# Loading the second tile of an early output projection ahead of the values, and pacing the first tile closer, in a hybrid attention layer

## The chip, the cores and the metric

The kernel runs on one NeuronCore of one Trainium2 chip. The metric is the device time of one execution in microseconds (us). The profile is one execution, seen from its first to its last instruction (the span). Engines: PE multiplies (PEld loads its weights), DVE, ACT and POOL work element by element, SP issues most DMAs.

## The reference

One decoder layer on x of 1024 tokens by 1024 channels, in float32. A normalised input goes through one wide projection. Eight differential-attention heads and four gated-linear-attention (GLA) heads use its columns, and their outputs (2048 columns together) go through the output projection.

```python
h = rms_norm(x, pre_g)
z = jnp.einsum('bsd,de->bse', h, w_in)
qa, ka, va, ga, qb, kb, vb, gb, gk_low = split_columns(z)
...
# per attention head: two softmax maps over causal scores
p = jax.nn.softmax(jnp.where(mask, s, -jnp.inf), axis=-1)
w = p[:, :, 0] - lam * p[:, :, 1]
out = jnp.einsum('bhqk,bkhv->bqhv', w.astype(v.dtype), v)
...
oa = rms_norm(oa, subln_g) * (1.0 - lam_init)
oa = oa.reshape(B, S, DA_WIDTH) * jax.nn.silu(ga)
ob = gla_chunked(...)
ob = rms_norm(ob, gla_g).astype(x.dtype)
ob = ob.reshape(B, S, GLA_WIDTH) * jax.nn.silu(gb)
y = jnp.einsum('bse,ed->bsd', jnp.concatenate([oa, ob], axis=-1), w_out)
return x + rms_norm(y, post_g)
```

## The kernel before

Every float32 operand is split into a high and a low part, and a product is three matmuls (high by high, low by high, high by low).

From 0 to about 624 us the kernel projects the input, runs the GLA heads in between, and writes their 1024 normalised columns, already split, to the scratch tensor `mixe` (a pair of 512 KB tiles for each block of 128 tokens). Queries, keys, values and gates of the attention heads go to scratch tensors too.

From 624 to about 922 us three streams of instructions are interleaved by `merge`:

- `all_scores` walks through the heads and, in a head, through the query blocks from 7 down to 0. Block qb has (qb+1)*128 keys and two maps, and a map is cut at 512 keys into pieces. A piece is two matmuls (`sc<-k,q` and `sc<-ks,q`) into one of three PSUM banks, and one DVE instruction (`p<-sc,maskt`) that masks it and keeps the minimum in `stt`. Behind the last piece of a map comes the exponential on ACT (`p<-p,stt`). Behind the second map come a reciprocal on DVE, a product on POOL (`p<-p,stt,lam`), and the combination of the two maps on DVE (`p<-p,stt,p`). Only then are the block's weights done.
- `all_values` transposes the weights (`wtr` on PE, split by ACT and DVE into `wt_hi` and `wt_lo`) and multiplies them with the values (`po`). The first transposes of a half need the weights of four query blocks; those of a head's first half need blocks 7, 6, 5 and 4. The values of a head come by `load_v`.
- `out_early` is the part of the output projection that can be done early. First the eight tiles of the GLA columns (`ypart<-wo_hi,m_hi` and so on): a tile is one block of 128 tokens, two halves of the output columns (dh) and eight steps of three matmuls, 48 matmuls in all. Each finished half goes by ACT (`yst<-ypart`) and a DMA to the scratch tensor `yd`. The last of these tiles waits until seven gated outputs are stored. Behind them come eight tiles of the first four attention heads, one for each of `ENDS`, and then the start of heads 4 to 6 for two blocks, whose operands `mix_pair(0)` loads (`m_raw<-mixd`) and splits (`m_hi<-m_raw`, `m_lo<-m_raw`).

`merge` gives each stream a clock: a stream that yields a number moves its clock by that number times (end - begin)/cost, and the stream whose clock is lowest goes next. A stream may yield a condition instead, and then sits out until it holds. Matmuls keep the order that results. The other engines' instructions and DMAs that aren't pinned are put in order per queue by a scheduler, so a queue's order follows from the program only in part.

`mix(st)` loads the two parts of a GLA tile on SP into buffers of which there are two of each, so a load waits until the matmuls of the tile before last have read theirs. Loads of tiles 0 and 1 are pinned in program order. From 922 us to the end the rest of the projection, the last norm and the residual follow (`yps`).

Of the kernel before, what the change touches and what calls it, by code (L numbers as in the profile page):

```python
# [17 lines left out]
NT = S // P  # L18
KT = D // P
HB = 4  # L20
DA_HEADS = 8
# [10 lines left out]
def hymba_kernel(  # L32
# [44 lines left out]
    def fp(t):  # L77
        return t.bitcast(F32)
# [974 lines left out]
    E, wo = D // P, {}  # L1053
    md = mixd.rearrange("(e p) s -> p e s", p=P)

    def weights(e):
        i = e % 8
        wo[e] = [
            hw.tile(
                [P, D], F32R, tag=f"{('h11', 'h12', 's1', 'h22')[i // 2]}_{n}{i % 2}", name=f"wo_{n}"  # L1060
            )
            for n in ("hi", "lo")
        ]
        engine = sp if e < E else pool
        for t in range(2):
            ins = engine.dma_start(fp(wo[e][t]), wod[e][t])
            if e >= E:
                tc.keep_in_program_order(ins)
# [3 lines left out]
    def mix_tiles():  # L1072
        n_mix[0] += 1
        return [
            hw.tile([P, 8, P], F32R, tag=f"s2_{n}{n_mix[0] % 2}", name=f"m_{n}")
            for n in ("hi", "lo")
        ]

    def mix(st):

        part = mix_tiles()
        for t in range(2):
            ins = sp.dma_start(fp(part[t]), mixe[st, t])
            if st < 2:
                tc.keep_in_program_order(ins)
        return part
# [44 lines left out]
    stored, last_mix = [], {}  # L1131
# [9 lines left out]
    def load_v(h):  # L1141
        v = [smp.tile([P, NT, P], F32R, tag="v", name=f"v{t}", bufs=4) for t in range(2)]
        for t in range(2):

            with tc.issue_after(qk_load[0]) if h else nullcontext():
                ins = sp.dma_start(fp(v[t]), v_d[h // 4][h % 4, t])
            if h == 0:
                tc.keep_in_program_order(ins)
        return v

    v_first = load_v(0)

    n_sc, n_tr = [0], [0]
# [216 lines left out]
    def load_mix(st, e, n, pool_d=None):  # L1370
        rows = slice(st * P, (st + 1) * P)
        if pool_d:
            raw = pool_d.tile([P, 4, P], F32, tag="m_raw", name="m_raw", bufs=4)
        else:
            raw = wop.tile([P, 4, P], F32, tag="m_raw", name="m_raw", bufs=4)
        mix_load[:] = [sp.dma_start(raw[:, :n, :], md[:, e : e + n, rows]).ins]
        return raw

    def mix_part(st, e, n, raw=None, pool_d=None):

        raw = load_mix(st, e, n, pool_d) if raw is None else raw
        if pool_d:
            hi, lo = (
                pool_d.tile([P, 4, P], F32R, tag=f"m_{p}", name=f"m_{p}", bufs=4) for p in ("hi", "lo")
            )
        else:
            hi, lo = mix_tiles()
        pin(pool_d, act.copy(hi[:, :n, :], raw[:, :n, :]))
        dve.tensor_tensor(lo[:, :n, :], raw[:, :n, :], fp(hi[:, :n, :]), ALU.subtract)
        return hi, lo  # L1390
# [7 lines left out]
    def times(ps, part, e0, dh, e, last):  # L1398
        mh, ml = part
        hi, lo = wo[e]  # L1400
        for i, (a, b) in enumerate(((mh, hi), (ml, hi), (mh, lo))):
            mm(
                ps, a[:, e - e0, :], b[:, cols(dh)],
                start=(e == e0 and i == 0), stop=(e == last and i == 2),
            )

    def y_bank(st, dh, name):
        return bank(Y[dh], [P, 512], name)

    def y_tile(ps):  # L1410
        y = smp.tile([P, 512], F32, tag="yst", name="yst", bufs=2)
        act.copy(y, ps)
        return y

    def out_early():

        part = mix0
        ps = [y_bank(0, dh, "ypart") for dh in range(2)]
        for e in range(E, E + 8):
            yield 1.0  # L1420
            if e == E:
                nxt = mix(1)
            for dh in range(2):
                times(ps[dh], part, E, dh, e, E + 7)
            yield 1.0
        for dh in range(2):
            sp.dma_start(yd[0][dh], y_tile(ps[dh]))
        for st in range(1, NT - 1):
            part, nxt = nxt, mix(st + 1)
            rows = slice(ENDS[st - 1] * P, ENDS[st - 1] * P + P)  # L1430
            sp.dma_start(out[0, rows, :], x[0, rows, :])
            for dh in range(2):
                ps = y_bank(st, dh, "ypart")
                for e in range(E, E + 8):
                    times(ps, part, E, dh, e, E + 7)
                    yield 0.69
                sp.dma_start(yd[st][dh], y_tile(ps))

        yield lambda: len(stored) >= 7
        part = nxt  # L1440
        ps = [y_bank(NT - 1, dh, "ypart") for dh in range(2)]
        raws_o = [load_mix(st, 0, 4) for st in ENDS[:3]]
        for e in range(E, E + 8):
            for dh in range(2):
                times(ps[dh], part, E, dh, e, E + 7)
                yield 0.69
            if e < E + 4:
                weights(e - E)
            if e == E + 6:
                nxt = mix_part(ENDS[0], 0, 4, raws_o.pop(0))  # L1450
        for dh in range(2):
            kept = sp.dma_start(yd[NT - 1][dh], y_tile(ps[dh]))
        for n, st in enumerate(ENDS):
            part = nxt
            if n == 1:
                yield lambda: len(stored) >= 8
            if n + 3 < NT:
                raws_o.append(load_mix(ENDS[n + 3], 0, 4))

            if 1 <= n <= 4:  # L1460
                with tc.issue_after(kept.ins), tc.issue_after(mix_load[0]):
                    weights(3 + n)
            if n + 1 < NT:
                nxt = mix_part(ENDS[n + 1], 0, 4, raws_o.pop(0))
            for dh in range(2):
                ps = y_bank(st, dh, "ypart")
                for e in range(4):
                    times(ps, part, 0, dh, e, 3)
                    yield 0.69
                pool.dma_start(yd[st][dh], y_tile(ps), accum_op=ALU.add)  # L1470
        yield lambda: len(stored) >= 2 * (DA_HEADS - 1) - 1
        mix_pair(0)
        for n, st in enumerate(ENDS[:2]):
            if n:
                yield lambda: scored
            for dh in range(2):
                seed(st, dh, (Y, SC)[n][dh], sums_of(n)[:, dh])
            yield 0.7
        for st in ENDS[:2]:
            for dh in range(2):  # L1480
                for e in range(4, 7):
                    last_times(st, dh, parts_d[st], e)
                    yield 0.69
            if st == ENDS[0]:
                mix_pair(2)
                seed(ENDS[2], 0, SC[2], sums_of(2)[:, 0])
# [3 lines left out]
    def sums_of(n):  # L1490


        if n not in sums_so_far:
            yp = sums_so_far[n] = kp.tile([P, 2, 512], F32, tag=("k0", "ks0", "q0")[n], name="yp")
            for dh in range(2):
                sp.dma_start(yp[:, dh], yd[ENDS[n]][dh])
        return sums_so_far[n]

    def mix_pair(n):

        hi, lo = (t.rearrange("p (a b) c -> p a b c", b=4) for t in mix_tiles())
        for i, st in enumerate(ENDS[n : n + 2]):
            raw = load_mix(st, 4, 3)
            act.copy(hi[:, i, :3], raw[:, :3])
            dve.tensor_tensor(lo[:, i, :3], raw[:, :3], fp(hi[:, i, :3]), ALU.subtract)
            parts_d[st] = hi[:, i], lo[:, i]
# [25 lines left out]
    def seed(st, dh, b, yp):  # L1532
        open_bank(b)
        ps = ps_d[st, dh] = opened.pop(b, None) or bank(b, [P, 512], "yps")
        opened[b] = None
        pin(b not in Y, act.copy(ps, yp))

    def last_times(st, dh, part, e):
        mh, ml = part
        hi, lo = wo[e]  # L1540
        for i, (a, b) in enumerate(((mh, hi), (ml, hi), (mh, lo))):
            mm(
                ps_d[st, dh], a[:, e - 4, :], b[:, cols(dh)],
                start=False, stop=(e == 7 and i == 2), skip_group_check=True,
            )

    T = 8 * 36.0
    LAG, SOON = 34.0, 2.0
# [4 lines left out]
    merge(  # L1553
        [0.0, T, DA_HEADS * s_cost, all_scores()],
        [LAG - SOON, T + LAG, DA_HEADS * 10.0 * (1 + SOON / T), all_values()],
        [-6.0, T + LAG + 20, 16.0 + 14 * 5.52 + 16 * 2.76 + 11.8, out_early()],
    )


# [122 lines left out]
```

## Time and profile before

| | us |
|---|---|
| median of 3 runs | 973.23 |
| lowest and highest run | 973.07, 973.25 |
| span of the profiled execution, first to last instruction | 971.1 |
| PE busy (of the span) | 958.7 (99%) |
| PEld busy | 814.5 (84%) |
| DVE busy | 735.5 (76%) |
| ACT busy | 604.6 (62%) |
| POOL busy | 207.9 (21%) |

For the profiled execution only the span is known. It is 2.1 us below the median of the runs, and what lies around it (before the first and after the last instruction) is in the runs' times alone. Matmuls overlap in a pipeline, so a matmul's start says more than its end.

### The profile page before, as it was taken

The numbers are of one execution on the slowest core, as the hardware profiler recorded it, in microseconds if no ns is written. First come the engines' busy times: TensorE is split into PE (matmuls) and PEld (weight loads), VectorE is DVE, ScalarE is ACT, GpSimd is POOL, SyncE is SP. The second block draws the span as 40 slices with busy tenths as digits, with TensorE's granted clock in tenths as the row PEclk, the third lists the DMA queues.
The fourth block names the chain that finished last, engine by engine and source line by source line (L and its number), as shares of the span: only waits on it lengthen the run. The fifth ranks groups of instructions, "written<-read, shape, count | busy, mean of one in ns | idle before, by whom it ended". The sixth has DMA issues, their size and how long they took to land.

```text
span 971.1 us, 15096 instructions
## 1 busy us (share of the span) xinstructions
PE 958.7 (99%) x4977; PEld 814.5 (84%) x4977; DVE 735.5 (76%) x1464; ACT 604.6 (62%) x1166; POOL 207.9 (21%) x266
## 2 busy tenths in 40 slices
PE   8999999999999999999999999999999999999997
PEld 7998988888888888888888888878888888888786
DVE  5996698897687686686766576587888888898554
ACT  8752364764667555576665344366786787887773
POOL 4300001212141221231100002121322222443322
PEclk9999999999999999999999999999999999999999
DMA  9433366578568987986754588996656769994777
GB/s 347 163 103 117 101 192 225 170 239 294 199 210 255 300 272 251 302 277 212 259 177 152 163 251 269 401 336 203 221 170 218 241 200 355 334 286 106 152 210 148
DMA packets 151293, 220.39 MB, mean 227 GB/s; under 512 B 15728, under 2 KB 86384, under 8 KB 151120
## 3 DMA queue, kind: packets, MB, share of 16 engines
q1 hardware_dynamic: 137056, 178.70, 56.8%
q0 software_dynamic: 14160, 40.74, 14.5%
q8 instruction: 39, 0.64, 0.3%
q14 instruction: 38, 0.31, 0.1%
HBM read 133.93 MB, written 88.60 MB: 229 GB/s over the span
## 4 chain that ended last, share of the span: by engine, by line
PE 94%; ACT 3%; DVE 1%; issue 1%; DMA 0%; POOL 0%; DVEq 0%; ACTq 0%; POOLq 0%
PE x L142 23%; PE z L142 16%; PE y L142 16%; PE ypart L142 13%; PE sc L142 7%; PE po L142 5%; PE yps L142 4%; PE wtr L145 3%; PE gpo L142 3%; PE kv L142 1%; ACT junk L66 1%; PE gkl_ps L142 1%; PE pa L142 1%; DVE p L66 1%; ACT h_hi L66 0%
## 5 line engine op out<-in xcount | busy, mean ns | idle before, releaser
L66 ACT CAST w<-w_raw 128x512 fp32r<-128x512 f32 (+1 forms) x150 | 98.0, 655 | 92.3 <-PE y L142 46.4
L66 DVE TENSOR_TENSOR w<-w_raw,w 128x512 fp32r<-128x512 f32 (+1 forms) x150 | 109.3, 732 | 48.8 <-ACT w L66 44.6
L66 ACT ACTIVATE p<-p,stt 128x896 f32<-128x896 f32 (+7 forms) x128 | 99.3, 777 | 36.2 <-DVE stt L66 35.2
L66 ACT COPY s<-x 128x512 f32<-128x512 f32 x82 | 47.8, 586 | 88.8 <-PE x L142 88.2
L66 POOL TENSOR_SCALAR p<-p,stt,lam 128x1024 f32<-128x1024 f32 (+3 forms) x64 | 56.2, 879 | 147.7 <-DVE stt L66 143.8
L66 DVE CUSTOM_DVE_ANT_0 p<-sc,maskt 128x512 f32<-128x512 f32 (+3 forms) x128 | 74.3, 585 | 14.2 <-PE sc L142 12.9
L66 POOL DMA_DIRECT2D wo_d<-wo_hi x32 | 17.5, 545 | 313.9 <-ACT wo_hi L66 313.9
L142 PE MATMUL z<-s_hi,w 128*128 128x512 f32 x320 | 80.2, 393 | 0.0
L142 PE MATMUL x<-s_hi,w 128*128 128x512 f32 x320 | 80.1, 392 | 0.0
L142 PE MATMUL y<-h_hi,w 128*128 128x512 f32 x320 | 80.0, 392 | 0.0
L142 PE MATMUL ypart<-wo_hi,m_hi 128*128 128x512 f32 x192 | 79.5, 414 | 0.1
L142 PE MATMUL ypart<-wo_hi,m_lo 128*128 128x512 f32 x192 | 75.5, 393 | 0.0
L142 PE MATMUL ypart<-wo_lo,m_hi 128*128 128x512 f32 x192 | 75.4, 393 | 0.0
L142 PE MATMUL sc<-k,q 128*128 128x512 f32 (+1 forms) x192 | 69.1, 363 | 1.4 <-DVE stt L66 1.3
L142 PEld LDWEIGHTS z<-s_hi,w 128*128 128x128 f32 x320 | 59.7, 188 | 12.3
L142 PEld LDWEIGHTS y<-h_hi,w 128*128 128x128 f32 x320 | 59.7, 188 | 12.3
L142 PEld LDWEIGHTS x<-s_hi,w 128*128 128x128 f32 x320 | 59.7, 188 | 12.3
L66 DVE TENSOR_TENSOR w_raw<-w_raw 128x512 f32<-128x512 f32 (+1 forms) x88 | 66.1, 751 | 1.9 <-DMA w_raw<-in_w_in_dram 0.8
L142 PE MATMUL sc<-ks,q 128*128 128x512 f32 (+1 forms) x192 | 66.0, 347 | 0.0
L66 ACT CAST wt_hi<-wtr 128x512 fp32r<-128x512 f32 (+1 forms) x80 | 42.8, 535 | 25.1 <-PE wtr L145 24.3
L66 DVE TENSOR_TENSOR wt_lo<-wtr,wt_hi 128x512 fp32r<-128x512 f32 (+1 forms) x80 | 50.6, 633 | 8.9 <-ACT wt_hi L66 8.2
L66 DVE TENSOR_TENSOR c<-z,s 128x512 f32<-128x512 f32 x48 | 32.8, 688 | 30.6 <-ACT s L66 20.3
(225 smaller groups left out, 2351.7 us busy)
## 6 DMA issues: line engine op xcount, KB each, us to landing
w_raw<-in_w_in_dram SPq DMA_DIRECT2D x48, 512.0 KB, 4.9
wo_d<-wo_hi POOLq DMA_DIRECT2D x32, 256.0 KB, 3.8
q<-q_d SPq DMA_DIRECT2D x32, 256.0 KB, 4.7
k<-k_d SPq DMA_DIRECT2D x32, 256.0 KB, 5.5
ks<-k_d SPq DMA_DIRECT2D x64, 128.0 KB, 6.0
v<-v_d SPq DMA_DIRECT2D x16, 512.0 KB, 7.0
wo_raw<-in_w_out_dram POOLq DMA_DIRECT2D x31, 256.0 KB, 4.8
wo_d<-gqd POOLq DMA_DIRECT2D x22, 256.0 KB, 4.2
```

The source lines that it names most:

```text
L66: ins = op(*a, **k)
L142: tc.keep_in_program_order(pe.matmul(*a, **k))
L145: tc.keep_in_program_order(pe.transpose(dst, src, ident))
```

## The change

Four edits:

- The load of tile 1's GLA columns (`mix(1)`) stands ahead of the load of head 0's values, instead of behind the first step of tile 0. Both are pinned on SP.
- The steps of tile 0 yield 0.8 twice instead of 1.0 twice, so the clock of `out_early` moves on less with each.
- The cost of that stream is lowered by the same 3.2, so its later steps of 0.69 move the clock a little more than before (348 us over 146.04 instead of over 149.24).
- `mix_pair(0)` and its condition stand ahead of the last tile of the first four heads, instead of behind it.

```diff
+    mix1 = mix(1)
     v_first = load_v(0)
...
         for e in range(E, E + 8):
-            yield 1.0
-            if e == E:
-                nxt = mix(1)
+            yield 0.8
             for dh in range(2):
                 times(ps[dh], part, E, dh, e, E + 7)
-            yield 1.0
+            yield 0.8
+        nxt = mix1
...
             if n == 1:
                 yield lambda: len(stored) >= 8
+            if n == NT - 1:
+                yield lambda: len(stored) >= 2 * (DA_HEADS - 1) - 1
+                mix_pair(0)
...
-        yield lambda: len(stored) >= 2 * (DA_HEADS - 1) - 1
-        mix_pair(0)
...
-        [-6.0, T + LAG + 20, 16.0 + 14 * 5.52 + 16 * 2.76 + 11.8, out_early()],
+        [-6.0, T + LAG + 20, 12.8 + 14 * 5.52 + 16 * 2.76 + 11.8, out_early()],
```

The number of matmuls is the same. What moves is their order. On PE at the start of the interleaved stage (`sc` are score pieces of head 0's block 7, `ypart` steps of tile 0) there stood before, from the end of the first six `ypart` on:

```order
L142 MATMUL ypart_6198<-wo_lo_5969,m_hi_6028 128x512
L142 MATMUL sc_6212<-k0_5952,q1_5946 128x512
L142 MATMUL sc_6212<-ks0_5960,q1_5946 128x512
L142 MATMUL ypart_6197<-wo_hi_5972,m_hi_6028 128x512
L142 MATMUL ypart_6197<-wo_hi_5972,m_lo_6029 128x512
L142 MATMUL ypart_6197<-wo_lo_5973,m_hi_6028 128x512
L142 MATMUL ypart_6198<-wo_hi_5972,m_hi_6028 128x512
L142 MATMUL ypart_6198<-wo_hi_5972,m_lo_6029 128x512
L142 MATMUL ypart_6198<-wo_lo_5973,m_hi_6028 128x512
L142 MATMUL sc_6222<-k1_5949,q1_5946 128x512
L142 MATMUL sc_6222<-ks1_5955,q1_5946 128x512
```

And now, from the end of the first twelve `ypart` on:

```order
L142 MATMUL ypart_6202<-wo_lo_5973,m_hi_6028 128x512
L142 MATMUL sc_6218<-k0_5952,q1_5946 128x512
L142 MATMUL sc_6218<-ks0_5960,q1_5946 128x512
L142 MATMUL sc_6222<-k1_5949,q1_5946 128x512
L142 MATMUL sc_6222<-ks1_5955,q1_5946 128x512
L142 MATMUL sc_6227<-k0_5952,q1_5946 128x512
L142 MATMUL sc_6227<-ks0_5960,q1_5946 128x512
L142 MATMUL sc_6231<-k1_5949,q1_5946 128x512
L142 MATMUL sc_6231<-ks1_5955,q1_5946 128x512
L142 MATMUL ypart_6201<-wo_hi_5976,m_hi_6028 128x512
```

Twelve `ypart` stand ahead of the first score piece instead of six, the four pieces of block 7 stand together, and twelve more `ypart` follow them. On PE just ahead of the first transposes of head 0 (`wtr`, which read the weights of blocks 4, 5, 6 and 7) there stood before:

```order
L142 MATMUL sc_6385<-k0_5952,q0_5965 128x384
L142 MATMUL sc_6385<-ks0_5960,q0_5965 128x384
L142 MATMUL sc_6390<-k0_5952,q0_5965 128x384
L142 MATMUL sc_6390<-ks0_5960,q0_5965 128x384
L142 MATMUL ypart_6409<-wo_hi_5968,m_hi_6199 128x512
L142 MATMUL ypart_6409<-wo_hi_5968,m_lo_6200 128x512
L142 MATMUL ypart_6409<-wo_lo_5969,m_hi_6199 128x512
L145 MATMUL wtr_6413<-ident_71,p0_6312 128x128
```

And now:

```order
L142 MATMUL sc_6406<-k0_5952,q0_5965 128x384
L142 MATMUL sc_6406<-ks0_5960,q0_5965 128x384
L142 MATMUL ypart_6358<-wo_hi_5980,m_hi_6190 128x512
L142 MATMUL ypart_6358<-wo_hi_5980,m_lo_6191 128x512
L142 MATMUL ypart_6358<-wo_lo_5981,m_hi_6190 128x512
L142 MATMUL sc_6414<-k0_5952,q0_5965 128x384
L142 MATMUL sc_6414<-ks0_5960,q0_5965 128x384
L142 MATMUL ypart_6358<-wo_hi_5984,m_hi_6190 128x512
L142 MATMUL ypart_6358<-wo_hi_5984,m_lo_6191 128x512
L142 MATMUL ypart_6358<-wo_lo_5985,m_hi_6190 128x512
L145 MATMUL wtr_6425<-ident_71,p0_6318 128x128
```

Tile 1 (`ypart_6409` before, `ypart_6358` now) has had five of its steps of three matmuls by then instead of one; the same score pieces stand ahead of the transposes in both. On SP, in the same stretch, there stood before (`m_hi`, `m_lo` are the GLA tiles, `k_6344`, `q_6341`, `ks_6347` the loads of head 1 for its keys and queries 512 to 1023, each of the four parts of `ks` 128 KB):

```order
L1146 DMA v_6190<-v_d 128x1024
L1146 DMA v_6191<-v_d 128x1024
L1083 DMA m_hi<-mixe 128x1024
L1083 DMA m_lo<-mixe 128x1024
L1031 DMA k_6352<-k_d 128x512 x2
L1034 DMA ks_6355<-k_d 64x512 x4
L1031 DMA k_6344<-k_d 128x512
L1031 DMA q_6341<-q_d 128x512 x2
L1031 DMA k_6344<-k_d 128x512
L1034 DMA ks_6347<-k_d 64x512 x4
L1427 DMA y_d<-yst 128x512 x2
```

And now (`k_6365`, `q_6362`, `ks_6368` are those loads of head 1):

```order
L1083 DMA m_hi<-mixe 128x1024
L1083 DMA m_lo<-mixe 128x1024
L1146 DMA v_6194<-v_d 128x1024
L1146 DMA v_6195<-v_d 128x1024
L1031 DMA k_6373<-k_d 128x512 x2
L1034 DMA ks_6376<-k_d 64x512 x4
L1083 DMA m_lo<-mixe 128x1024
L1427 DMA y_d<-yst 128x512
L1083 DMA m_hi<-mixe 128x1024
L1031 DMA q_6362<-q_d 128x512
L1427 DMA y_d<-yst 128x512
L1031 DMA q_6362<-q_d 128x512
```

Tile 1's load stands ahead of the values, and tile 2's load and the two stores of tile 0 stand ahead of these loads of head 1 instead of behind them.

## The prediction

> **What bounds the kernel now.** I read the page first, its chain, then PE's waits, then the start of the interleaved stage in order of time.
>
> ```profile
> PE 958.7 (99%) x4977; PEld 814.5 (84%) x4977; DVE 735.5 (76%) x1464; ACT 604.6 (62%) x1166; POOL 207.9 (21%) x266
> ...
> PE 94%; ACT 3%; DVE 1%; issue 1%; DMA 0%; POOL 0%; DVEq 0%; ACTq 0%; POOLq 0%
> ```
>
> PE bounds: the chain that ended last lies on it for 94%. The number of matmuls stays, so only PE's waits can be won or lost. PE's waits from 600 us to the end, and the windows of the stage's start:
>
> ```profile
> PE sc L142 <- DVE stt L66: 1.3, 2, 1.1
> PE po L142 <- ACT wt_hi L66: 0.5, 1, 0.5
> PE wtr L145 <- DVE p L66: 0.4, 1, 0.4
> ```
>
> ```profile
> 624.00:632.00 8.00, 7.89 (x35) 6.22 (x35) 5.04 (x13) 3.12 (x5) 0.00 (x0) 1.00 0.99 349
> 632.00:640.00 8.00, 6.70 (x32) 5.18 (x30) 6.40 (x19) 3.30 (x6) 2.29 (x2) 1.00 0.88 268
> 640.00:647.00 7.00, 6.55 (x32) 5.14 (x32) 5.94 (x20) 5.74 (x13) 1.94 (x3) 1.00 1.02 372
> ```
>
> The columns after the length are busy time of PE, PEld, DVE, ACT, POOL, then clock, DMA share and GB/s. PE is idle for 0.11 + 1.30 + 0.45 = 1.86 us here; behind 650 us the only wait listed is `po`'s 0.5. But a matmul's busy time hides the time for which the next is late. PE's rows, by their starts:
>
> ```profile
> 624.99 0.50 PE L142 MATMUL ypart<-wo_hi,m_hi 128*128 128x512 f32 x1
> ...
> 638.64 0.28 PE L142 MATMUL sc<-ks,q 128*128 128x128 f32 x1
> 640.04 0.50 PE L142 MATMUL sc<-k,q 128*128 128x512 f32 x1 [1.12 <-DVE stt L66]
> ...
> 645.80 0.39 PE L142 MATMUL ypart<-wo_lo,m_hi 128*128 128x512 f32 x1
> 646.59 0.66 PE L145 MATMUL wtr<-ident,p 128*128 128x128 f32 x4 [0.40 <-DVE p L66]
> ```
>
> Here `wtr` starts 0.79 behind a matmul that needs 0.23. I add up what PE has to do from the first `ypart` to the first `wtr`. Prices come from the chain of waits:
>
> ```profile
> 624.99 0.98 PE ypart L142 x3
> 625.97 0.47 PE sc L142 x2
> 626.44 1.38 PE ypart L142 x6
> ```
>
> A step of three `ypart` takes 0.69. Tile 0's 48 and tile 1's first 3 are 17 steps, 11.7 us. The score pieces ahead of `wtr` are 12 pairs of 512 columns, 4 of 384, 2 of 256, 2 of 128; with 0.46 a pair and less in proportion that is 5.5 + 1.4 + 0.5 + 0.2 = 7.6. The first `ypart` started at 624.0, so 22.6 us passed for 19.3 of work: 3.3 us of waiting, nearly all there is behind 620. The chain here doesn't run on PE but through block 7, 6, 5, 4 on DVE, ACT and POOL.
>
> **The change, part by part.** *Closer pace.* By the order, four more steps of tile 1 stand ahead of the first `wtr`: 4 x 0.69 = 2.76 us of work that PE no longer has behind it. What it brings is 2.76 less the time by which `wtr` comes later. For that I follow the softmax of the four blocks. DVE and its partners before:
>
> ```profile
> 628.31 0.75 DVE L66 CUSTOM_DVE_ANT_0 p<-sc,maskt,stt 128x512 f32<-128x512 f32 x1 [1.14 <-PE sc L142]
> ...
> 628.99 0.69 DVE L66 CUSTOM_DVE_ANT_0 p<-sc,maskt 128x512 f32<-128x512 f32 x1
> ...
> 629.83 0.75 DVE L66 CUSTOM_DVE_ANT_0 p<-sc,maskt,stt 128x512 f32<-128x512 f32 x1
> ...
> 631.03 0.69 DVE L66 CUSTOM_DVE_ANT_0 p<-sc,maskt 128x512 f32<-128x512 f32 x1 [0.45 <-PE sc L142]
> ...
> 633.93 1.29 DVE L66 SCALAR_TENSOR_TENSOR p<-p,stt,p 128x1024 f32<-128x1024 f32 x1 [0.76 <-POOL p L66]
> 635.13 0.61 DVE L66 CUSTOM_DVE_ANT_0 p<-sc,maskt,stt 128x384 f32<-128x384 f32 x1
> ...
> 638.43 1.15 DVE L66 SCALAR_TENSOR_TENSOR p<-p,stt,p 128x896 f32<-128x896 f32 x1 [0.25 <-POOL p L66]
> ...
> 641.86 0.35 DVE L66 CUSTOM_DVE_ANT_0 p<-sc,maskt,stt 128x128 f32<-128x128 f32 x1
> 642.92 1.02 DVE L66 SCALAR_TENSOR_TENSOR p<-p,stt,p 128x768 f32<-128x768 f32 x1 [0.70 <-POOL p L66]
> ...
> 645.65 0.88 DVE L66 SCALAR_TENSOR_TENSOR p<-p,stt,p 128x640 f32<-128x640 f32 x1
> ```
>
> ```profile
> 642.31 0.83 ACT L66 ACTIVATE p<-p,stt 128x640 f32<-128x640 f32 x1 [0.25 <-DVE stt L66]
> ```
>
> ```profile
> 644.72 0.88 POOL L66 TENSOR_SCALAR p<-p,stt,lam 128x640 f32<-128x640 f32 x1 [1.84 <-DVE stt L66]
> ```
>
> A second piece follows its first by 0.84 (it needs its `stt`), another map's by 0.68.
> - Block 7: six more `ypart` put the first score 1.38 later. Its four pieces then stand together, and DVE no longer waits the 1.14 for PE: the fourth piece begins 0.4 later than 629.83.
> - Block 6: now twelve `ypart` (2.76) stand between block 7's last score (ends 629.1) and block 6's first. Its first piece reaches DVE at 629.1 + 2.76 + 0.65 = 632.5 instead of 631.03, 1.5 later.
> - Both maps of block 6 now stand ahead of block 7's combination, which starts at 635.4 instead of 633.93; but at its end the piece of 635.13 is done too, so DVE is 0.9 late. Block 6's combination comes at 638.1, 0.3 early, with one more piece of block 5 behind it: block 5's last piece is 0.9 late.
> - Block 4: its last piece stands behind block 5's combination (643.3, 0.94 long) and starts at 644.2 instead of 641.86, 2.3 late. Its exponential on ACT starts 2.3 behind 642.31. The copies of tile 0 on ACT (0.59 each) fit before and between. Before, POOL's product came 1.6 behind that exponential's end at 643.1, because DVE stood in other work ahead of the reciprocal; now the reciprocal waits on ACT alone, and POOL starts at 645.8, 1.1 behind 644.72. Combination 646.75, `wtr` 647.7.
>
> So `wtr` comes 1.1 late, and 2.76 - 1.1 = 1.65 us are won; PE's wait there falls from 3.3 to 1.65. The bounds: if `wtr` keeps its time, 2.76 is won; if all 2.3 of block 4's lateness comes through, 0.45. I take 1.65, the end of the walk.
>
> The Trainium skill (Perfetto Trace Analysis, Identifying the Most-Contended Engine) says that matmul busy time misjudges PE since matmuls overlap. The rows agree: 1.86 idle by busy time, 3.3 by starts. By busy time no gain over 1.86 would be possible here; by starts 2.76 is.
>
> *Tile 1's load ahead of the values.* SP's rows:
>
> ```profile
> 634.39 1.08 SPq L1146 DMA_DIRECT2D v<-v_d x2
> 635.51 0.43 SPq L1083 DMA_DIRECT2D m_hi<-mixe  x1
> 635.98 0.43 SPq L1083 DMA_DIRECT2D m_lo<-mixe  x1
> ...
> 641.11 0.33 SPq L1031 DMA_DIRECT2D k<-k_d  x1
> ...
> 644.13 2.37 SPq L1034 DMA_DIRECT2D ks<-k_d  x4
> ```
>
> Values are issued 1 us later and land 1 to 4 us later, near 643; `po` first reads them behind `wtr`. Cost 0. Tile 1 starts at 643.0 instead of 645.3, and its load, issued at 634.4, has 8 us. Behind it the loads of head 1 lose their place: tile 2's load and two stores stand ahead, and the first store waits for ACT's copy (643.0). The queries issue at 644.1 and `ks` at 646.4 instead of 644.13. What needs them, and how long they take:
>
> ```profile
> 652.27 0.46 PE sc L142 x2
> ```
>
> ```profile
> ks<-k_d SPq DMA_DIRECT2D x2, 128.0 KB, 4.7
> ```
>
> The score at 652.27 needs the first two `ks`, issued by 646.9 now and landing at 651.6; PE gets there at 647.7 + 5.2 = 652.9. Cost 0, with 1.3 us to spare.
>
> *Lower cost.* Later steps are spaced 2% wider, so PE's lead of four steps shrinks to none over 275 us, about 0.35 us a head. Cost 0 while DVE has slack; it waits for PE often enough (700 to 740 us):
>
> ```profile
> DVE p L66 <- PE sc L142: 3.3, 4, 1.0
> ```
>
> *`mix_pair(0)` earlier.* The order of ACT and DVE hardly moves: both casts stay behind the copy of the same tile, and what changes is that one cast of `wt_hi` (384 columns) now stands behind them.
>
> ```profile
> 909.22 0.51 ACT L66 CAST m_hi<-m_raw 128x384 fp32r<-128x384 f32 x1 [0.52 <-DMA m_raw<-mixd]
> 910.09 0.48 ACT L66 CAST wt_hi<-wtr 128x384 fp32r<-128x384 f32 x1 [0.36 <-PE wtr L145]
> ...
> 911.97 0.60 PE L145 MATMUL wtr<-ident,p 128*128 128x128 f32 x4
> ```
>
> That cast and DVE's behind it then end near 910.8; the next to want the bank is the `wtr` of 911.97. Nothing won or lost: 0, between a loss of 0.5 if the load is 1.7 late and a gain of 0. The wait of 0.5 for `wt_hi` at 920 stays.
>
> Sum: -1.65, span 971.1 - 1.65 = 969.45; on the runs, 2.1 above the span, 973.23 - 1.65 = 971.6.
>
> **The rivals.**
> 1. *`wtr` keeps its time.* For it: DVE has gaps. Against: twelve `ypart` stand ahead of block 6. 973.23 - 2.76 = 970.5.
> 2. *The lead is missed later.* If the softmax has no slack in later heads, each of the four steps comes back as a wait: 971.6 + 2.76 = 974.4, slower. For it: the lead does shrink to none. Against: DVE's waits for PE above.
> 3. *SP's order holds up head 1.* Ahead of its `ks` now lie tile 2 (1.05 MB) and two stores (0.5 MB):
>
> ```profile
> DMA packets 468, 0.92 MB, mean 385 GB/s; under 512 B 63, under 2 KB 63, under 8 KB 468
> ```
>
> At this rate (641 to 643.4 us) 1.55 MB are 4.0 us, `ks` lands at 655.7, PE waits 2.8: 974.4, slower. It decides from a landing of 6.0 us on; from 7.6 on the kernel is slower than before. Against: nothing is issued from 640.2 to 642.9, so the queues drain. The Trainium skill (DMA: Bandwidth & Descriptors, Issuing engines are not separate DMA queues) says that all DMAs interleave on the same 16 engines; the share of 1.02 above agrees that they are full here.
> 4. *The third edit does nothing*, whatever the rest: that is in the sum.
>
> **How the numbers follow.** The forecast (971.0 to 972.4) gets 0.52, rival 1 (below 971.0) 0.22, rivals 2 and 3 0.13 each. 0.2% is 1.95 us, about what a measurement can tell: faster means below 971.28, all of rival 1 and 0.11 of the forecast, 0.33; slower, above 975.18, takes more than a price of rival 2 or 3 alone, 0.05; same 0.62. The range is from rival 1 with 0.5 for small waits elsewhere, 970.0, to rivals 2 and 3, 974.4.
>
> **What would show it.** First `wtr` at 647.7 with 1.65 us of waiting ahead of it and five steps of tile 1 done; block 6's first piece on DVE at 632.5 behind a wait for PE; head 1's second score without a DMA wait near 653; later rows 1.65 earlier; `po`'s wait for `wt_hi` still 0.5. Wrong would be a `wtr` before 647 or behind 648.5, a wait of `sc` for `k_d` or `ks`, or new waits of PE for DVE between 660 and 900.

## The result and the profile after

The changed kernel takes 977.29 us (median of 5 runs, 976.26 to 978.81); the kernel before, run beside it, 973.23 (972.80 to 973.28). The ratio is 1.0043, with a 95% interval of 1.0031 to 1.0055: slower by 4.1 us, where 1.65 less was forecast and 974.4 was the range's end. The profiled execution (977.29) has a span of 975.6, 4.5 more than before.

PE's and the chain's lines on the page of the changed kernel:

```profile
PE 960.5 (98%) x4977; PEld 814.1 (83%) x4977; DVE 739.9 (76%) x1464; ACT 605.4 (62%) x1166; POOL 201.9 (21%) x266
PE 88%; DMA 4%; DVE 3%; ACT 2%; issue 1%; SPq 1%; POOL 0%; DVEq 0%; ACTq 0%; POOLq 0%
```

PE's share of the chain fell from 94% to 88%, and DMA and SP are on it now. PE's waits from 600 us to the end:

```profile
PE wtr L145 <- DVE p L66: 1.8, 1, 1.8
PE sc L142 <- DMA ks<-k_d: 1.4, 1, 1.4
PE sc L142 <- DVE stt L66: 1.3, 3, 0.8
PE po L142 <- ACT wt_hi L66: 0.5, 1, 0.5
PE wtr L145 <- DVE wt_lo L66: 0.4, 2, 0.2
```

To see where the time lies I add up, for every matmul, the time to the next one's start less what its columns need (0.443 ns each, 0.227 us for 512). The waits are in that sum, and so are the small losses of transposes and restarts, which both kernels have.

| window, us | before | after | difference |
|---|---|---|---|
| 620 to 650.5 | 4.46 | 2.91 | -1.55 |
| 650.5 to 662 | 0.60 | 2.58 | +1.98 |
| 662 to 800 | 13.27 | 13.53 | +0.26 |
| 800 to 830 | 3.08 | 4.07 | +0.99 |
| 830 to 888 | 5.35 | 5.58 | +0.23 |
| 888 to 900 | 1.04 | 3.08 | +2.04 |
| 900 to the end | 3.22 | 3.75 | +0.53 |

The gain at the start is there, but 0.4 of the 1.55 is an edge of the table: the first transposes come later now, and some of their small losses fall behind 650.5. Up to the first `wtr` the sum is 3.49 before and 2.43 now, so 1.06 is gained, and the place near 654 costs 1.6 instead of 1.98. Three places take the gain back.

**Near 654: SP.** The chain of waits of the changed kernel, in order of time (start, length, what):

```profile
646.36 0.28 SPq L1427
...
648.63 0.45 SPq L1034
649.13 6.24 DMA ks<-k_d
655.37 0.04 issue
655.41 0.50 PE sc L142
```

The store of tile 0's second half (L1427) leaves SP at 646.3, behind it queries and keys, and the first `ks` (L1034) at 648.63. It stood at 644.13 before. The transfer takes 6.24, and PE waits 1.36 for it.

**Near 814: SP, then DVE.** The loads of `m_raw` on SP, before and after, and what DVE and PE then do in the changed kernel:

```profile
803.59 1.47 SPq L1376 DMA_DIRECT2D m_raw<-mixd  x3
```

```profile
805.84 2.91 SPq L1377 DMA_DIRECT2D m_raw<-mixd  x3
...
814.46 0.69 DVE L66 TENSOR_TENSOR m_lo<-m_raw,m_hi 128x512 fp32r<-128x512 f32 x1 [2.37 <-DMA m_raw<-mixd]
815.06 0.48 DVE L66 CUSTOM_DVE_ANT_0 p<-sc,maskt,stt 128x256 f32<-128x256 f32 x1
...
815.61 0.50 PE L142 MATMUL sc<-k,q 128*128 128x512 f32 x1 [0.80 <-DVE stt L66]
```

`m_raw` leaves 2.3 later: a second pair of weights and two `ks` now stand ahead of it. Its loads also take longer, 7.6 from issue to landing (median) instead of 5.1. `m_lo` stands at the head of DVE's queue and waits 2.37 for it; the piece that would free a score bank stands behind `m_lo`.

**Near 894: ACT.** Here the last head's block 4 is late. ACT, DVE and PE of the changed kernel:

```profile
889.04 0.59 ACT L66 COPY o<-po 128x512 f32<-128x512 f32 x1 [0.27 <-PE po L142]
889.66 0.63 ACT L66 ACTIVATE fold<-o 64x512 f32<-64x512 f32 x1
890.32 0.63 ACT L66 ACTIVATE sq<-o 64x512 f32<-64x512 f32 x1
890.86 0.81 ACT L66 ACTIVATE p<-p,stt 128x640 f32<-128x640 f32 x1
...
894.99 0.88 DVE L66 SCALAR_TENSOR_TENSOR p<-p,stt,p 128x640 f32<-128x640 f32 x1
...
895.93 0.66 PE L145 MATMUL wtr<-ident,p 128*128 128x128 f32 x4 [1.80 <-DVE p L66]
```

Before, that exponential stood ahead of the copy of `o`:

```profile
886.15 0.83 ACT L66 ACTIVATE p<-p,stt 128x640 f32<-128x640 f32 x1
886.89 0.19 ACT L66 ACTIVATION_READ_ACCUMULATOR p<-p,stt 128x1 f32 x1
886.98 0.57 ACT L66 COPY o<-po 128x512 f32<-128x512 f32 x1
```

On PE the `po` of head 6 had moved ahead of one step of the projection, and on ACT the copy of its result now stands ahead of the exponential. That the one led to the other was not tested by itself.

### The profile page after: what moved, and what is told of

Same layout as the page of the kernel before. It is cut to its first block, busy times and chain, and to the rows that moved or that the text cites. A ratio compares the mean times of both kernels' runs of the same rounds, so it can differ in the third digit from the quotient of the medians.

```text
span 975.6 us, 15098 instructions
## 1 busy us (share of the span) xinstructions
PE 960.5 (98%) x4977; PEld 814.1 (83%) x4977; DVE 739.9 (76%) x1464; ACT 605.4 (62%) x1166; POOL 201.9 (21%) x266
## 4 chain that ended last, share of the span: by engine, by line
PE 88%; DMA 4%; DVE 3%; ACT 2%; issue 1%; SPq 1%; POOL 0%; DVEq 0%; ACTq 0%; POOLq 0%
PE x L142 23%; PE z L142 16%; PE y L142 16%; PE ypart L142 10%; PE sc L142 6%; PE yps L142 4%; PE po L142 4%; PE gpo L142 3%; PE wtr L145 3%; DVE p L66 2%; DMA ks<-k_d 1%; PE kv L142 1%; DMA m_raw<-mixd 1%; DMA w_raw<-in_w_in_dram 1%; PE gkl_ps L142 1%
## 5 line engine op out<-in xcount | busy, mean ns | idle before, releaser
L66 ACT ACTIVATE p<-p,stt 128x128 f32<-128x128 f32 (+7 forms) x128 | 99.3, 777 | 42.6 <-DVE stt L66 41.0
L66 DVE SCALAR_TENSOR_TENSOR p<-p,stt,p 128x1024 f32<-128x1024 f32 (+3 forms) x64 | 53.9, 843 | 4.0 <-POOL p L66 3.8
```

Source lines behind the costliest of these rows:

```text
L66: ins = op(*a, **k)
```

## The experiments

In all runs the ratio is to the kernel before, run beside it on the same chip, with its 95% interval. The diffs show the lines that matter; `...` stands for lines left out.

**The parts alone.** TensorE's order is set by the pace and the cost alone: with only the load or only the casts moved it is that of before.

> Only tile 1's load stands ahead of the values; pace, cost and the casts are as before. TensorE's order is that of before, word for word. Order theory (the closer pace and the lower cost lose the time by the order they set; the load and the casts are worth nothing): 973.2 +- 0.5, no wait of sc for ks. Load theory (the values and head 1's loads come late because tile 1 goes first): at least 1.5 slower, 974.7 or more, with a wait of sc for ks near 652.

```diff
+    mix1 = mix(1)
     v_first = load_v(0)
...
-            if e == E:
-                nxt = mix(1)
...
+        nxt = mix1
```

Measured 973.02, ratio 0.9999 (0.9990 to 1.0007). As the order theory says.

> The closer pace and the lower cost alone: tile 1 is loaded behind the values as before, the casts of mix_pair(0) stand where they stood. TensorE's order is that of the changed kernel. Order theory: 977.3 +- 1.0, with the waits of the changed kernel: sc for ks near 653 (1.4), sc behind a late m_raw near 814 (0.8), wtr for p near 894 (1.8). Load theory: 973 to 974, without the wait for ks.

```diff
-            yield 1.0
+            yield 0.8
...
-        [-6.0, T + LAG + 20, 16.0 + 14 * 5.52 + 16 * 2.76 + 11.8, out_early()],
+        [-6.0, T + LAG + 20, 12.8 + 14 * 5.52 + 16 * 2.76 + 11.8, out_early()],
```

Measured 977.36 (975.48 to 981.79), ratio 1.0048 (1.0032 to 1.0064). The whole loss, without the load and the casts, and the waits of the changed kernel but for the one at 814, which this execution lacks; in its place `ms` waits 0.6 for DVE's `sq_hl` near 842.

> Only mix_pair(0) stands ahead of the last early tile. TensorE's order is that of before. Order theory: 973.2 +- 0.5. Rival (the casts lose time on ACT and DVE at the last heads): 974.2 or more, with a new wait of PE between 890 and 922.

```diff
+            if n == NT - 1:
+                yield lambda: len(stored) >= 2 * (DA_HEADS - 1) - 1
+                mix_pair(0)
...
-        yield lambda: len(stored) >= 2 * (DA_HEADS - 1) - 1
-        mix_pair(0)
```

Measured 973.09, ratio 0.9998 (0.9989 to 1.0006). Nothing.

**The lead kept to the end.**

> The changed kernel with the stream's cost at 16.0 again: the lead of four to five steps is kept to the end instead of shrinking to none. Order theory: the last head's first exponential of block 4 stands ahead of the copy of o on ACT again, so the wait of wtr for p near 894 (1.8 to 2.0) goes, and the wait for ks near 653 stays: 975.3 +- 0.8. Rival (the lead itself is what each later wait takes back, whatever the order on ACT): 977.3 or more, with the wait of wtr for p still 1.5 or more.

```diff
-        [-6.0, T + LAG + 20, 12.8 + 14 * 5.52 + 16 * 2.76 + 11.8, out_early()],
+        [-6.0, T + LAG + 20, 16.0 + 14 * 5.52 + 16 * 2.76 + 11.8, out_early()],
```

Measured 978.42, ratio 1.0059 (1.0046 to 1.0071): a miss. The wait at 894 is gone as expected, and so is the one for `ks`, which was expected to stay, but others stand in their place. PE's waits of this run:

```profile
PE yps L142 <- ACT m_hi L66: 2.3, 1, 2.3
PE wtr L145 <- DVE p L66: 1.0, 1, 1.0
```

The projection's steps were done early, the scores were not, and at 928 PE had nothing left to fill its wait for the last head. Behind 900 this run loses 3.7 more by starts than the changed kernel. The old cost doesn't help, so the lowered cost by itself is not what loses the time, and the lead that is kept to the end comes back as a wait there.

**Each place mended by itself.** All three keep the changed kernel's pace and cost.

> The changed kernel, but tile 2 is loaded behind head 1's keys and queries on SP (in the middle of tile 1) instead of ahead of them. Theory of separate places (the closer pace shifts the orders of other queues, and each of three places costs by itself: ks behind tile 2 on SP, 1.5 us; m_raw behind the weights on SP, 0.8 us; the last head's exponential behind the copy of o on ACT, 2.0 us): sc waits for no DMA near 653, and 977.3 - 1.5 = 975.8 +- 0.7. Rival (one bound: the scores of each head are late by the lead, and a wait taken away comes back at the next place): 977.3 +- 0.5, with the waits at 814 and 894 longer by what was won.

```diff
+                    if h == 0:
+                        ks1[:] = qk_load
...
-            part, nxt = nxt, mix(st + 1)
+            part = nxt
+            if st > 1:
+                nxt = mix(st + 1)
...
+                if st == 1 and dh == 1:
+                    with tc.issue_after(ks1[0]):
+                        nxt = mix(2)
```

(`ks1` holds the last of head 1's first `ks` loads.) Measured 975.96, ratio 1.0033 (1.0020 to 1.0045): 1.3 better than the changed kernel's 977.29, and no wait of PE for a DMA in the profile. The two ratios were measured beside different runs and their intervals overlap, so this run alone does not show the gain; the pair of runs below does. The wait at 894 stayed at 1.8, no longer than it was.

> The changed kernel, but on SP the three loads of m_raw stand ahead of the weights of the first heads. Separate places: the wait of sc behind the late m_raw near 814 (1.0) shrinks to the 0.25 of before or less, 976.5 +- 0.7. Rival (one bound): 977.3 +- 0.5 or slower, with the wait at another place.

```diff
             if e < E + 4:
-                weights(e - E)
+                with tc.issue_after(mix_load[0]):
+                    weights(e - E)
```

Measured 979.41, ratio 1.0062 (1.0048 to 1.0075): a miss. The wait at 814 is halved (0.51 by starts against 1.02), but the casts moved up on ACT and DVE, and `ms` waits 1.3 for DVE's `sq_hl` near 843. The profiled execution was the longest (981.64), and in it the wait for `ks` was 1.8. So what this order costs in a typical execution is known from the median alone.

> The changed kernel, but the copy of head 6's o stands behind the last head's exponential of block 4 on ACT, as it did before. Separate places: the wait of wtr for p near 894 (1.8) goes to 0.4 or less, 977.3 - 1.7 = 975.6 +- 0.7. Rival (one bound): the wait stays over 1.2, or an equal one comes behind 896; 977.3 +- 0.5.

```diff
+                    if (h, qb, m) == (DA_HEADS - 1, 4, 1):
+                        exp4[:] = [ins.ins]
...
+                with tc.issue_after(exp4[0]) if (h, half) == (DA_HEADS - 2, 1) else nullcontext():
-                act.copy(o, po)
+                    act.copy(o, po)
```

(`exp4` holds the last head's second exponential of block 4.) Measured 977.77 (976.03 to 979.16), ratio 1.0046 (1.0033 to 1.0058). In the profile the wait at 894 is gone (it was 1.97 by starts; now 0.20 at 905 and 0.48 at 911), yet the median didn't fall: waits for `ks`, `k` and `q` of 2.0 together stood in the profiled execution (979.16, the longest), and these change from one execution to the next.

> The changed kernel with all three mends of order (keys ahead of tile 2, m_raw ahead of the weights, the exponential ahead of o). Separate places: the sum, 977.3 - 1.5 - 0.8 - 1.7 = 973.3 +- 1.0, level with before; what is left of the lead's gain (1.1 at the first wtr) is taken by the waits of 0.4 at 735 and 877. Rival (one bound): 976 or more.

Measured 975.87, ratio 1.0029 (1.0017 to 1.0040): 2.6 short of the sum, and no better than the keys alone. In the profile the waits for `ks`, at 814 and at 894 are gone, but there is a new one, near 838 and again near 908:

```profile
PE ms L142 <- DVE sq_hl L66: 1.7, 2, 1.3
```

> The changed kernel with two mends: keys ahead of tile 2, and the last head's exponential ahead of the copy of o. Separate places: 975.96 (keys first alone) less 1.3 to 1.8 = 974.4 +- 0.6. Rival (the wait moves on to the norm of the next half): within 0.4 of 975.96, with a wait of ms for sq_hl of 1 or more near 838 or 908.

Both edits shown above, without the one for `m_raw`. Measured 974.56, ratio 1.0015 (1.0007 to 1.0024): 1.40 below the run with the keys alone, as expected, and 1.31 below the run with all three. With the late keys out of the way, the mend at 894 shows its worth, so the places at 654 and 894 add up. But the new wait is here too:

```profile
PE ms L142 <- DVE sq_hl L66: 1.2, 2, 0.9
```

The place at 814 is not one by itself. At this pace, where the wait of `sc` near 814 is short or absent, `ms` waits for `sq_hl` some 25 us later. By starts, the profiled execution of the changed kernel loses 9.6 between 800 and 888, and those with the pace alone, with the keys first and with these two mends 9.4, 10.0 and 9.9; in the two with `m_raw` moved up it is 10.8 and 10.9, and before it was 8.4. So moving `m_raw` up did not lessen what is lost there.

**The lead given back where it does no harm.** With cost 16.0 and 3.2 paid out over tiles 1 to 6, TensorE's order from the gated last tile on is that of before. In all of the runs from here on, but for the one that says otherwise, tile 2 is loaded behind the keys as above.

> Keys ahead of tile 2 on SP, and the lead given back before the gated last tile: the cost is 16.0 again, and each half of tiles 1 to 6 yields 0.267 more, 3.2 together, so from about 800 us on TensorE's order is that of before. Theory (the lead is a gain of 1.2 up to 800 us, and what loses the time is the shifted order of the three streams in heads 5 to 7): the waits behind 820 are those of before (only po for wt_hi), 973.0 - 1.2 = 971.8 +- 0.6, faster than before. Rival (the lead is taken back by waits wherever it is paid): 973.0 or more, with waits of PE between 660 and 820 that sum to 1.2 or more.

```diff
                 sp.dma_start(yd[st][dh], y_tile(ps))
+                yield 3.2 / (2 * (NT - 2))
...
-        [-6.0, T + LAG + 20, 12.8 + 14 * 5.52 + 16 * 2.76 + 11.8, out_early()],
+        [-6.0, T + LAG + 20, 16.0 + 14 * 5.52 + 16 * 2.76 + 11.8, out_early()],
```

Measured 972.53 (972.26 to 972.70), ratio 0.9995 (0.9986 to 1.0003): 0.1 above the range that was expected, and not told apart from before. The losses behind 800 are gone: by starts 2.80, 5.38, 1.05 and 3.27 in the last four windows of the table, those of before but for 0.3 less in the first. But between 662 and 800, where the lead is paid back, 1.1 more is lost than before, nearly all that the start had won. 0.84 of it is one wait at 733. DVE, POOL and PE there:

```profile
728.38 1.21 POOL L66 TENSOR_SCALAR p<-p,stt,lam 128x1024 f32<-128x1024 f32 x1 [3.52 <-DVE stt L66]
...
728.55 1.57 DVE L66 TENSOR_TENSOR sq_hl<-sq,sq_hl 64x512 fp32r<-64x512 f32 x1 [0.34 <-ACT sq_hl L66]
...
732.50 0.69 DVE L66 TENSOR_TENSOR wt_lo<-wtr,wt_hi 128x512 fp32r<-128x512 f32 x1
...
733.34 0.52 PE L145 MATMUL wtr<-ident,p 128*128 128x128 f32 x3 [0.68 <-DVE wt_lo L66]
```

> As the run with the lead given back in small parts, but with tile 2 ahead of head 1's keys on SP as in the changed kernel. Theory: the wait for ks comes back in most executions, 1.0 to 2.0 slower than that run: 972.8 to 973.8. Rival (the late keys only cost when the lead is lost anyway): the same time as that run, within 0.4.

The same without the mend of the keys: 974.27 (973.19 to 978.71), ratio 1.0019 (1.0008 to 1.0029). The order on SP alone is worth 1.7 here, with intervals that do not overlap, and the times spread by 5.5 between the shortest and the longest, against 0.4. The profiled execution is the shortest, without a wait for `ks`; that the late keys make the long ones is inferred. The two longest (976.64 and 978.71) have granted clocks of 0.996 and 0.995, all the others 0.998 or 0.999.

> Keys ahead of tile 2, cost 16.0, and the whole 3.2 given back in one yield just ahead of the gated last tile, near 795. Theory: the four or five score steps that then stand together wait for DVE, 0.69 of filler each is missing: between 971.8 and 973.5, with waits of sc for DVE near 800. Rival (DVE has slack enough there): as the run with small parts, within 0.4.

```diff
+        yield 3.2
         yield lambda: len(stored) >= 7
...
```

975.81, ratio 1.0036 (1.0023 to 1.0049), worse than expected: the scores that then stand together fill DVE's queue (it is busy for 3.97 of the 4.00 us from 798), and PE waits for the squares behind them.

```profile
802.42 0.77 PE L142 MATMUL ms<-sq_hl,ones 128*128 128x512 f32 x1 [2.36 <-DVE sq_hl L66]
```

**The last wait, and more lead.**

> The run with the lead given back in small parts and the keys first, and on DVE the low part of head 2's squares (sq_hl) ahead of the reciprocal that starts POOL's product of head 3's block 7. Theory (sq_hl takes 1.57 instead of 0.69 because POOL's product runs beside it; the 0.88 comes out at PE as the wait of wtr for wt_lo near 733): sq_hl 0.69, the wait of 0.84 gone, 972.5 - 0.8 = 971.7 +- 0.4, faster than before. Rival (sq_hl is slow for another reason, or the wait is the length of DVE's work there): sq_hl stays over 1.2, or the wait stays over 0.5 and the time within 0.3 of 972.5.

```diff
+        split[:] = [dve.tensor_tensor(hl[64:], sq[:64], fp(hl[:64]), ALU.subtract).ins]
...
+                    with tc.issue_after(split[0]) if (h, qb) == (3, NT - 1) else nullcontext():
-                    dve.reciprocal(st[:, 4:6], st[:, 2:4])
+                        dve.reciprocal(st[:, 4:6], st[:, 2:4])
```

(`split` holds DVE's latest `sq_hl`.) Measured 972.08 (971.49 to 972.53) against 973.11, ratio 0.9987 (0.9978 to 0.9996): faster than both kernels, by 1.0 and by some 5. Against the run without this edit (972.53) it is 0.45 less, with intervals that overlap. DVE and POOL now:

```profile
729.22 0.68 DVE L66 TENSOR_TENSOR sq_hl<-sq,sq_hl 64x512 fp32r<-64x512 f32 x1 [0.75 <-ACT sq_hl L66]
...
730.30 1.21 POOL L66 TENSOR_SCALAR p<-p,stt,lam 128x1024 f32<-128x1024 f32 x1 [4.79 <-DVE stt L66]
...
731.51 0.69 DVE L66 TENSOR_TENSOR wt_lo<-wtr,wt_hi 128x512 fp32r<-128x512 f32 x1
```

The wait at 733 is gone. The combination also moved behind `wt_lo` in DVE's order, so the run doesn't tell how much of the 0.84 (by starts, all won back) was POOL's and how much that. A wait of 0.6 for `ks` is in this profile too: the keys still land late in some executions.

> As that run, with tile 0 paced at 0.7 (four times 1.2 more is given back over tiles 1 to 6, 4.8 in all): 72 early matmuls stand ahead of the first wtr instead of 66 or, in before, 51. Theory (the scores are late by what stands ahead of them, so more lead adds work in front of the first wtr and wins at most what PE still waits there, 1.2): within 0.5 of the other run, and the first wtr 0.7 to 1.4 later. Rival (each step of lead is worth its 0.69): 970.7 or less.

The pace 0.7 and 4.8 to give back: 974.90, ratio 1.0018 (1.0009 to 1.0027). Neither theory: 2.8 worse. The first `wtr` starts at 651.97 instead of 648.86; 1.4 of that is the six more matmuls ahead of it, and 1.7 is time that PE loses before it by starts, for late scores and for ACT's copy of a finished half. Another 1.1 is lost between 800 and 830. The waits of the whole run:

```profile
PE sc L142 <- DVE stt L66: 1.8, 3, 1.2
PE ypart L142 <- ACT yst L66: 0.8, 1, 0.8
```

## Why the prediction was wrong, step by step

- *Closer pace, -1.65.* The mechanism was right, the size too large: 1.06 by starts up to the first `wtr`. The walk held row by row: block 6's first piece on DVE at 632.52 (632.5 was written), block 4's product on POOL at 645.95 (645.8), its combination at 646.86 (646.75), done at 647.75. But the first `wtr` came at 648.24 instead of 647.7, 1.65 later than before and not 1.1, and 2.76 less 1.65 is 1.1. It didn't wait for the weights: PE still had its own steps to finish. The walk followed the weights to the end and took for granted that PE would be there; PE's losses ahead of `wtr` fell from 3.49 to 2.43, where 3.3 to 1.65 was written, and among the 2.43 are two waits of `sc` near 640 of 0.44 and 0.42.
- *Tile 1 ahead of the values, and the casts: 0 each.* Right: 973.02 and 973.09 alone, and without both of them 977.36 against the 977.29 with all edits.
- *"Cost 0, with 1.3 us to spare" for head 1's loads.* This step failed, and it is rival 3's mechanism. `ks` was put at 646.4 and a landing after 4.7. It left at 648.63, because stores and loads ahead of it each waited in SP's queue, and landed after 6.24, at 655.37; rival 3 had written 655.7. Both errors were needed: issued by 649.1, a landing after 4.7 would still have come at 653.8, and PE could have begun at 653.9. The 4.7 was the median of two transfers in a stretch of 1.7 us; the page of the kernel before has 6.0 over its 64 `ks`, the very bound from which the prediction let this rival decide. Putting tile 2 behind the keys won 1.7 in the pair of runs that shows it clearly, and 1.3 by the medians of the other.
- *"Lower cost. Cost 0 while DVE has slack."* This step failed too, and it cost the most. DVE's waits for PE between 700 and 740 are slack on the average. They don't say that a given row of a queue can come two steps of projection earlier against the scores. In heads 5 to 7 the shift turned the order round on SP (weights ahead of `m_raw`) and on ACT (`o` ahead of the exponential). Between 800 and 900 that cost 3.3 by starts, near rival 2's 2.76, but not as four steps that each came back as a wait: with the order of before from 800 on, nothing came back there. That the copy of `o` ahead of the exponential is one cause is shown (1.4, and the wait gone); for the loss between 800 and 888 it is only shown that it goes with the shifted order.
- *The chances.* Rivals 2 and 3 were priced as alternatives, 974.4 each, with 0.05 for slower. They have different causes and both came: by the table, with 1.98 near 654 and 4.05 from 662 on, against 1.55 won, the sum is 4.48, the span's 4.5.

What was not settled: the wait for `ks` differs from execution to execution, also with the keys first, and no run tells what in the transfers makes it so. For the loss between 800 and 888 no mend was found at the changed kernel's pace.

## What to carry to other kernels

A lead of one stream over another is worth what the engine waited at the place where it is taken, and has to be paid back; choose the place of the payment, and make the order behind it the one that is known to run well. Whoever changes a rate in a merge can change every later row of every queue: compare the orders of the DMA queue and of the helper engines to the end, and look at each transfer or cast that came ahead of something on the path. A wait that a mend removes is worth its length only if no other takes its place: add up the loss over the whole stretch. When two rivals have different causes, their prices can add.

## What the runs showed of the hardware

**The granted clock halves at some waits.** In the run with the pace alone (its profiled execution, 981.79, is its longest) PE waited 0.78 and 1.26 around 655. PE's rows after that, and the windows (busy time of PE, PEld, DVE, ACT, POOL, then granted clock, DMA share, GB/s):

```profile
656.88 0.80 PE L142 MATMUL sc<-ks,q 128*128 128x512 f32 x1 [1.26 <-DMA ks<-k_d]
657.48 0.63 PE L142 MATMUL ypart<-wo_hi,m_hi 128*128 128x512 f32 x1
657.90 0.63 PE L142 MATMUL ypart<-wo_hi,m_lo 128*128 128x512 f32 x1
658.33 0.63 PE L142 MATMUL ypart<-wo_lo,m_hi 128*128 128x512 f32 x1
```

```profile
650.00:655.00 5.00, 4.37 (x27) 3.51 (x25) 5.00 (x19) 4.13 (x12) 1.22 (x2) 1.00 1.06 348
657.00:660.00 3.00, 3.00 (x8) 2.31 (x9) 1.18 (x4) 1.24 (x2) 0.00 (x0) 0.50 0.84 273
```

Starts are 0.43 apart instead of 0.23, at a granted clock of 0.50. In this trace the clock stays there for 3.41 us from 656.91 on, and every other such fall ahead of the last 10 us of the kernel is as long: at 802.05, in the wait of 2.36 in the run with the lead given back at once; at 932.32, behind waits of 2.32 and 0.34 with the old cost; near 656.8 in two more runs, at waits for keys of 0.56 and 1.81 (`m_raw` first) and of 0.85 and 0.97 (the exponential first). In 3.41 us at half the clock PE does the work of 1.7, so a fall can cost 1.7 on top of the wait. The three longest of the profiled executions (979.16, 981.64 and 981.79) all have one near 657.

Not every such wait brings it. In the changed kernel's profile the waits of 1.36 and 1.80 were not followed by it; the run with the pace alone waited 1.83 at the place of the 1.80, and there the clock fell at 899.25. The Trainium skill (TensorE: Matmul & The Clock Gate, Why this matters for your kernels) puts the limit at gaps of about 3 us; here 2.36 in one piece was enough, and once 1.83. No run varied the length of a wait by itself.

**POOL holds up DVE.** `sq_hl` takes 0.69 in most places and 1.57 where POOL's product of 1024 columns began 0.17 ahead of it; when its order was changed so that it ran first, it took 0.68. The Trainium skill (SBUF — State Buffer, SBUF: two separate sides) says that a DVE operation with two SBUF inputs and a POOL operation that reads SBUF share a pair of ports, which whoever starts first holds for its whole instruction. The trace agrees: the product ended at 729.59 and `sq_hl` at 730.12, 0.53 later. In the kernel before, `sq_hl` took 1.57 at 763.32, where a product began 0.17 ahead, and 0.88 at 728.17, 799.41 and 834.40, where it began 0.86 ahead, and each time it ended 0.53 or 0.54 behind the product. In the changed kernel it took 1.03 at 893.45, ahead of the combination for which PE waits near 894.
